# Gate and up projections of an encoder layer as seven block products instead of eight, with one pool of weight operands

## The chip, the cores and the metric

The kernel runs on one core of one Trainium2 chip. The time is the device time of one execution in microseconds (us); a kernel's time is the median of its runs. One execution was also taken by the hardware profiler, which gives each engine's instructions with start, duration and what released them. The engines are PE (TensorE: matmuls and transposes), DVE (VectorE), ACT (ScalarE), POOL (GpSimd) and SP (SyncE, which issues the DMA transfers). PEld is the loading of a matmul's stationary operand, which runs beside PE.

## The reference

One step of a streaming encoder layer for 640 tokens (512 of a prompt, 128 of eight samples), 1024 features, inner dimension 2816. What comes ahead of the change is attention; the tail is what the change touches:

```python
def layer_tail(x, ada, o_a, o_b, gates, w_o_a, w_o_b, w_out, g_norm_ffn, w_gate, w_up, w_down):
    shift1, scale1, gate1, shift2, scale2, gate2 = ada
    B, S = o_a.shape[:2]
    y_a = o_a.reshape(B, S, N_HEADS_A * V_DIM_A) @ w_o_a
    y_b = o_b.reshape(B, S, N_HEADS_B * HEAD_DIM_B) @ w_o_b
    x = x + gate1 * ((gates[:, :, 0] * y_a + gates[:, :, 1] * y_b) @ w_out)
    h = modulate(rmsnorm(x, g_norm_ffn), shift2, scale2)
    return x + gate2 * ((jax.nn.silu(h @ w_gate) * (h @ w_up)) @ w_down)
```

All tensors are fp32.

## The kernel before

Every large product is made of matmuls on pairs: an fp32 operand x is split into hi, a rounded copy that the matmul takes, and lo = x - hi. `split` (L83 to L89) makes the pair: ACT casts (L85), DVE subtracts (L86; POOL where the caller says so). `mm3` (L91 to L94) then issues three matmuls for one product, hi by hi, hi by lo, lo by hi. A `granule` (L178) is a weight piece of 128 partitions x 1024: SP loads it into a raw tile (three of them, tag w_raw), and `split` makes w_hi and w_lo (three of each in a pool).

The stages: conditioning terms, input projection and attention until about 594 us; the output projections of the two branches (L1086 to L1116), in four weight groups `bg`, until about 664; w_out with the residual (L1181 to L1201), two column halves c by five tiles of 128 tokens, until 721; the FFN from 726 to the end. Each stage's operands are in pools; `wstA` lives from the start, and `wstB2` beside it is opened after attention, so that the first `w_o_a` granule uses buffers of a pool that is open all along.

In the second column half of w_out, each token tile t goes through `h2_stats(t)` (L1140: sum of squares, reciprocal root, xn = x times it), then `h2_cols(t)` (L1149: eight transposes, scale and shift, split into h2T and h2Tl, the FFN's moving operands). Meanwhile the gate and up weights of FFN blocks 0 and 1 are loaded and split, with POOL making the lo part (`ff_weights(.., G)`).

The FFN goes through 22 blocks of 128 inner columns. `ff_block` (L1209) does one block for one half of the tokens (320 columns): 24 matmuls into a gate bank, silu on ACT (L1216), 24 into an up bank, a DVE product of the two (L1219), and a split into aT and aTl. A block takes 96 matmuls. The first two blocks do the first token half first, which does not need the last token tile. The blocks come in passes of 8, 8 and 6. After each pass the down projection adds to the residual (matmuls of 512 columns into one bank per tile and column half, L1250 and L1251 on DVE).

The order of each engine's instructions is fixed when the program is built, by a scheduler that mixes the stages where their operands allow; at run time each engine goes through its list in order and waits on semaphores. An engine that waits holds up all that stands behind it on its list.

Of the kernel before, what the change touches and what calls it, by code (L numbers as in the profile page):

```python
# [47 lines left out]
def layer_kernel(  # L48
# [42 lines left out]
    def mm3(out, lh, ll, rh, rl, start, stop):  # L91
        T.matmul(out, lh, rh, start=start, stop=False)  # L92
        T.matmul(out, lh, rl, start=False, stop=False)  # L93
        T.matmul(out, ll, rh, start=False, stop=stop)  # L94
# [67 lines left out]
    wa = ctx.enter_context(pool("wstA", side="right"))  # L162
# [884 lines left out]
    wb_cm = pool("wstB2", side="right")  # L1047
    wb = wb_cm.__enter__()
    AB = (wa, wb)
    gp_cm = pool("gatebc", side="right")  # L1050
    gp = gp_cm.__enter__()
# [12 lines left out]
    def gate_rows(c0, scale):  # L1064

        raw = ada_rows(c0)
        hi = wa.tile([P, 1024], F32R, tag="w_hi", bufs=3, name=nm("whi"))[0:19, :]
        lo = wa.tile([P, 1024], F32R, tag="w_lo", bufs=3, name=nm("wlo"))[0:19, :]
        split(hi, lo, raw)
        out = []  # L1070
        for v in range(2):
            g_ = gp.tile([P, DM], F32, tag=f"gate{v}", name=nm("gate"))
            for c in range(2):
                cc = slice(c * 512, (c + 1) * 512)
                ps = mm_tile()
                T.matmul(ps, selr[:, v * P:(v + 1) * P], hi[:, cc], start=True, stop=False)  # L1076
                T.matmul(ps, selr[:, v * P:(v + 1) * P], lo[:, cc], start=False, stop=True)  # L1077
# [4 lines left out]
    with pool("mwork") as mw:  # L1082
# [10 lines left out]
        for bg in range(4):  # L1093
            wo = [granule(AB[br], wo_v[br][:, :, bg * 256:(bg + 1) * 256], [4, 256]) for br in range(2)]
            for bl in range(2):
# [6 lines left out]
                for hf in range(2):  # L1102
                    c = slice(hf * HALF, (hf + 1) * HALF)
                    ts = []
                    for br in range(2):
                        ps = mm_tile()
                        for k in range(4):
                            ws = slice(bl * P, (bl + 1) * P)
                            mm3(ps[:, :HALF], wo[br][0][:, k, ws], wo[br][1][:, k, ws],
                                oS[br, hf][0][:, k, :], oS[br, hf][1][:, k, :], k == 0, k == 3)  # L1110
# [20 lines left out]
    h2T = h2p.tile([P, KD, NT], F32R, tag="h2T", name="h2T")  # L1131
    h2Tl = h2p.tile([P, KD, NT], F32R, tag="h2Tl", name="h2Tl")
# [4 lines left out]
    sq = ow.tile([P, 2, TT], F32, tag="sq", name="sq")  # L1137
    xns = {}
# [10 lines left out]
    def h2_cols(t):  # L1149
        tsl = slice(t * P, (t + 1) * P)  # L1150
        for b in range(2):
# [4 lines left out]
            hf_ = ow.tile([P, 512], F32, tag="hfull", bufs=2, name=nm("hfull"))  # L1156
# [14 lines left out]
            split(h2T[:, kb_, tsl], h2Tl[:, kb_, tsl], hf_.rearrange("p (k n) -> p k n", k=4))  # L1171
# [4 lines left out]
    def ff_weights(fb, eng=None):  # L1176
        cs_ = slice(fb * P, (fb + 1) * P)
        return granule(wa, wg_v[:, :, cs_], [KD, P], eng=eng) + granule(wb, wu_v[:, :, cs_], [KD, P], eng=eng)

    ffw = []  # L1180
# [128 lines left out]
```

## Time and profile before

| | |
|---|---|
| median of 3 runs | 1199.36 us (1196.3 to 1201.92) |
| profiled execution, its own time | 1195.43 us |
| its span in the trace | 1193.7 us |
| PE busy | 1163.5 us, 97% |
| DVE / ACT / POOL busy | 650.9 / 521.1 / 106.5 us (55 / 44 / 9%) |
| mean granted TensorE clock | 0.991 |
| DMA | 155.29 MB, mean 130 GB/s |

The span is cut into 40 slices; each digit is the busy share of a slice in tenths (9 is 90% or more). PEclk is the clock granted to TensorE in tenths of full speed (full is 2.4 GHz, half 1.2 GHz):

```profile
PE   8899999999999999999899998999999999999998
PEld 6578988999998788889699888999889999889996
DVE  4988555857887785555555256422343332433333
ACT  6766533446776664566643166322122222112210
POOL 2521001000000000112012221000000000000000
PEclk9999999999999999999989999999999999999999
```

Slices 25 to 40 are the FFN: PE is full, DVE and ACT have much room and POOL does nothing. A matmul's duration in the trace is longer than the distance between two starts, because matmuls overlap in the array; the pace of a stream is read from starts.

### The profile page before, as it was taken

The page shows a single profiled execution, that of the slowest core. Times are in us where ns is not written, and L with a number is a line of the kernel's source. Part 1 is how long each engine was busy: PE and PEld are TensorE (multiplying, and loading weights), DVE is VectorE, ACT ScalarE, POOL GpSimd, SP SyncE. Part 2 cuts the span into 40 slices and gives each one's busy share as a digit, 9 for nine tenths or more (in the row PEclk, how much of TensorE's full clock was granted, in tenths as well). Part 3 has the DMA queues.
Part 4 walks back from the last instruction along what each step waited for, and adds up shares of the span by engine and source line. Part 5 has one row for each costly group of instructions (what it writes and reads, how often), then busy time and mean ns, then how long its engine had stood idle before and what let it go on. Part 6 is the DMA issues. An engine that isn't in the chain of part 4 may idle for free. (4 is left out here: it accounts for less than half of the span.)

```text
span 1193.7 us, 19291 instructions
## 1 busy us (share of the span) xinstructions
PE 1163.5 (97%) x7427; PEld 1045.2 (88%) x7427; DVE 650.9 (55%) x1472; ACT 521.1 (44%) x1062; POOL 106.5 (9%) x188
## 2 busy tenths in 40 slices
PE   8899999999999999999899998999999999999998
PEld 6578988999998788889699888999889999889996
DVE  4988555857887785555555256422343332433333
ACT  6766533446776664566643166322122222112210
POOL 2521001000000000112012221000000000000000
PEclk9999999999999999999989999999999999999999
DMA  8732434567555445576676112322123222222211
GB/s 235 269 107 65 134 124 145 173 196 224 171 174 165 133 147 168 197 232 218 180 266 198 36 57 71 110 85 71 36 71 108 87 73 87 68 74 72 71 45 62
DMA packets 155166, 155.29 MB, mean 130 GB/s; under 512 B 24632, under 2 KB 115283, under 8 KB 155074
## 3 DMA queue, kind: packets, MB, share of 16 engines
q1 hardware_dynamic: 155074, 154.05, 41.6%
q8 instruction: 59, 0.97, 0.3%
q14 instruction: 33, 0.27, 0.1%
HBM read 135.15 MB, written 18.88 MB: 129 GB/s over the span
## 5 line engine op out<-in xcount | busy, mean ns | idle before, releaser
L85 ACT CAST whi<-wraw 128x1024 fp32r<-128x1024 f32 (+3 forms) x168 | 173.2, 1037 | 274.6 <-PE mm L94 108.0
L86 DVE TENSOR_TENSOR wlo<-wraw,whi 128x1024 fp32r<-128x1024 f32 (+3 forms) x152 | 182.5, 1203 | 134.4 <-ACT whi L85 131.3
L93 PE MATMUL mm<-h2Tl,whi 128*128 128x320 f32 x704 | 217.2, 309 | 0.0
L94 PE MATMUL mm<-h2T,wlo 128*128 128x320 f32 x704 | 217.1, 309 | 0.0
L92 PE MATMUL mm<-h2T,whi 128*128 128x320 f32 x704 | 216.8, 309 | 0.2 <-ACT h2T L85 0.2
L92 PEld LDWEIGHTS mm<-h2T,whi 128*128 128x128 f32 x704 | 131.9, 188 | 0.9 <-ACT h2T L85 0.4
L93 PEld LDWEIGHTS mm<-h2Tl,whi 128*128 128x128 f32 x704 | 132.1, 188 | 0.4 <-DVE h2Tl L86 0.3
L94 PEld LDWEIGHTS mm<-h2T,wlo 128*128 128x128 f32 x704 | 132.1, 188 | 0.0
L1219 DVE TENSOR_TENSOR sg<-mm,sg 128x320 f32<-128x320 f32 x44 | 21.6, 492 | 119.6 <-PE mm L94 117.5
L93 PE MATMUL mm<-wlo,aT 128*128 128x512 f32 x220 | 85.5, 389 | 0.0
L92 PE MATMUL mm<-whi,aT 128*128 128x512 f32 x220 | 85.5, 389 | 0.0
L94 PE MATMUL mm<-whi,aTl 128*128 128x512 f32 x220 | 85.4, 389 | 0.0
L92 PE MATMUL mm<-whi,hT_hi 128*128 128x512 f32 (+3 forms) x240 | 79.5, 332 | 2.5 <-ACT jk L320 2.5
L92 PE MATMUL mm<-hT_hi,whi 128*128 128x320 f32 x256 | 81.7, 319 | 0.0
L94 PE MATMUL mm<-whi,hT_lo 128*128 128x512 f32 (+3 forms) x240 | 79.6, 332 | 0.0
L94 PE MATMUL mm<-hT_hi,wlo 128*128 128x320 f32 x256 | 79.5, 311 | 0.0
L93 PE MATMUL mm<-hT_lo,whi 128*128 128x320 f32 x256 | 79.4, 310 | 0.0
L93 PE MATMUL mm<-wlo,hT_hi 128*128 128x512 f32 (+3 forms) x240 | 79.3, 331 | 0.0
L1250 DVE TENSOR_TENSOR tmp<-mm,gate 128x512 f32<-128x512 f32 x30 | 20.7, 691 | 79.9 <-PE mm L94 79.9
L85 ACT CAST aT<-sg 128x320 fp32r<-128x320 f32 x44 | 20.0, 455 | 77.2 <-DVE sg L1219 77.2
L92 PEld LDWEIGHTS mm<-whi,hT_hi 128*128 128x128 f32 x240 | 45.2, 188 | 6.5 <-ACT jk L320 2.9
L92 PEld LDWEIGHTS mm<-hT_hi,whi 128*128 128x128 f32 x256 | 48.2, 188 | 2.6 <-issue 1.7
(328 smaller groups left out, 2476.6 us busy)
## 6 DMA issues: line engine op xcount, KB each, us to landing
wraw<-in_w_ada_dram SPq DMA_DIRECT2D x48, 512.0 KB, 4.8
wraw<-in_w_in_dram SPq DMA_DIRECT2D x28, 512.0 KB, 4.6
wraw<-in_w_gate_dram SPq DMA_DIRECT2D x22, 512.0 KB
wraw<-in_w_up_dram SPq DMA_DIRECT2D x22, 512.0 KB, 3.9
wraw<-in_w_down_dram SPq DMA_DIRECT2D x22, 512.0 KB, 3.6
lat<-in_cache_kv_latent_dram SPq DMA_DIRECT2D x16, 512.0 KB, 5.7
wraw<-in_cache_band_v_dram SPq DMA_DIRECT2D x16, 512.0 KB, 5.2
kn<-in_cache_band_k_dram SPq DMA_DIRECT2D x16, 512.0 KB, 3.7
```

What stands on the lines that cost most here:

```text
L85: S.copy(hi, src)
L86: (eng or V).tensor_tensor(out=lo, in0=src, in1=f(hi), op=ALU.subtract)
L92: T.matmul(out, lh, rh, start=start, stop=False)
L93: T.matmul(out, lh, rl, start=False, stop=False)
L94: T.matmul(out, ll, rh, start=False, stop=stop)
L1219: V.tensor_tensor(out=sg, in0=pu[:, :HALF], in1=sg, op=ALU.mult)
L1250: V.tensor_tensor(out=tmp, in0=ps, in1=gate2[t // 4][:, cc], op=ALU.mult)
```

## The change

With the gate and up weights of one block as two rows of a 2x2 block matrix (gate over up; inner halves 1 and 2), and the activations as a 2x2 block matrix (inner halves by token halves), gate and up for all tokens are a 2x2 block product. It is done in seven products instead of eight. Each product has a weight operand of 128x512 and activations of 4 x 320 columns, so 12 matmuls; a block takes 84.

- The activations are kept as hB (three blocks: b11, b21, b22) and hS (four sums t1 to t4, made on POOL from each token tile, then split in four pieces of 128x1280 after the last tile). The two token halves are interleaved by 64 tokens within each tile.
- Per block POOL makes s1, s2, a21' and s4 from the raw weights (L1246 to L1249 of the new code), in one tile `sums`. Each of the seven operands is split on its own (ACT cast and DVE subtraction of 128x512).
- Partial results are shared between products in one PSUM bank: after a product into `pa`, ACT copies the bank (u1, u2, u3, L1260) and the next product adds on top of it. The tiles sums, u1, u2, u3 and u5 have one buffer each.
- All weights from the output projections on go through one pool, `wops`, with 12 pairs of 128x512 and the three raw tiles; the old pool is closed after attention. POOL no longer splits blocks 0 and 1; their weights are not loaded ahead by a call of their own. The rows of the last gate come ahead of the FFN. Passes are 6, 6, 6 and 4 blocks.

```diff
+    def mm3(out, lh, ll, rh, rl, start, stop, more=False):
...
     sb_cm.__exit__(None, None, None)
-    wb_cm = pool("wstB2", side="right")
-    wb = wb_cm.__enter__()
-    AB = (wa, wb)
+    wa_cm.__exit__(None, None, None)
+
+    wa = ctx.enter_context(pool("wops", side="right"))
+
+    def operand(src, n=512):
+        hi = wa.tile([P, 512], F32R, tag="op_hi", bufs=12, name=nm("ophi"))[:, :n]
+        lo = wa.tile([P, 512], F32R, tag="op_lo", bufs=12, name=nm("oplo"))[:, :n]
+        split(hi, lo, src)
+        return hi, lo
+
+    def operands(src, shape):
+        raw = load_raw(src, shape)[0]
+        return [operand(raw[:, i * 512:(i + 1) * 512]) for i in range(2)]
...
-            split(h2T[:, kb_, tsl], h2Tl[:, kb_, tsl], hf_.rearrange("p (k n) -> p k n", k=4))
+            quarter.append(hf_.rearrange("p (k a x) -> p a k x", k=4, a=2))
+        (b11, b12), (b21, b22) = [(h[:, 0], h[:, 1]) for h in quarter]
+        split(hB[0][:, 0, :, q], hB[1][:, 0, :, q], b11)
+        split(hB[0][:, 1, :, q], hB[1][:, 1, :, q], b21)
+        split(hB[0][:, 2, :, q], hB[1][:, 2, :, q], b22)
+        t1, t2, t3, t4 = [hT_[:, i, :, q] for i in range(4)]
+        for o, a, b in ((t1, b12, b11), (t2, b22, t1), (t3, b22, b12), (t4, b21, t2)):
+            G.tensor_tensor(out=o, in0=a, in1=b, op=ALU.subtract)
...
-                if t in (1, 3):
-                    ffw.append(ff_weights(len(ffw), G))
     h2_cols(4)
     mT_cm.__exit__(None, None, None)
+    tsum = ctx.enter_context(pool("tsum", side="right"))
+    hS = [tsum.tile([P, 4, 4, HALF], F32R, tag=f"hS{i}", name=f"hS{i}") for i in range(2)]
+    for i in (1, 0, 2, 3):
+        split(hS[0][:, i], hS[1][:, i], hT_[:, i])
...
+        def ff_block(fb, fi):
+            raw = ff_raw(fb)
+            (a11, a12), (a21, a22) = [(r[:, 0:512], r[:, 512:1024]) for r in raw]
+            sums = fw.tile([P, 3, 512], F32, tag="sums", name=nm("sums"))
+            s1, s2, s4 = sums[:, 0], sums[:, 1], sums[:, 2]
+            G.tensor_tensor(out=s1, in0=a21, in1=a22, op=ALU.add)
+            G.tensor_tensor(out=s2, in0=s1, in1=a11, op=ALU.subtract)
+            G.tensor_tensor(out=a21, in0=a11, in1=a21, op=ALU.subtract)
+            G.tensor_tensor(out=s4, in0=a12, in1=s2, op=ALU.subtract)
+
+            def product(bank, w, h, i, start=True):
+                wh, wl = operand(w)
+                for k in range(4):
+                    ks = slice(k * P, (k + 1) * P)
+                    mm3(bank[:, :HALF], wh[:, ks], wl[:, ks], h[0][:, i, k, :], h[1][:, i, k, :],
+                        start and k == 0, k == 3, not start)
+
+            def part(bank, tag):
+                o = fw.tile([P, HALF], F32, tag=tag, name=nm(tag))
+                S.copy(o, bank[:, :HALF])
+                return o
+
+            pa, pc, pb = mm_tile(), tr_tile(), (mm_tile if fb % 2 else tr_tile)()
+            product(pa, a11, hB, 0)
+            u1 = part(pa, "u1")
+            product(pc, a12, hB, 1)
+            V.tensor_tensor(out=u1, in0=pc[:, :HALF], in1=u1, op=ALU.add)
+            S.activation(out=u1, in_=u1, func=AF.Silu)
+            product(pa, s2, hS, 1, start=False)
+            u2 = part(pa, "u2")
+            product(pb, s1, hS, 0)
+            u5 = part(pb, "u5")
+            product(pa, a21, hS, 2, start=False)
+            u3 = part(pa, "u3")
+            G.tensor_tensor(out=u3, in0=u3, in1=u5, op=ALU.add)
+            product(pb, s4, hB, 2, start=False)
+            V.tensor_tensor(out=u2, in0=pb[:, :HALF], in1=u2, op=ALU.add)
+            S.activation(out=u2, in_=u2, func=AF.Silu)
+            product(pa, a22, hS, 3, start=False)
+            V.tensor_tensor(out=u1, in0=pa[:, :HALF], in1=u1, op=ALU.mult)
+            G.tensor_tensor(out=u2, in0=u2, in1=u3, op=ALU.mult)
+            for i, u in enumerate((u1, u2)):
+                o = [a[:, fi].rearrange("p (t a x) -> p t a x", a=2, x=64)[:, :, i, :] for a in (aT, aTl)]
+                split(o[0], o[1], u.rearrange("p (t x) -> p t x", x=64))
```

How the instructions stand on the engines, at three places. In the rows, a line number is followed by the operation, what it writes, what it reads, its shape, and the semaphores on which it waits.

First PE in the second pass of the FFN. Before, a block for one token half: the last matmuls into the gate bank (`mm_10555`), and the first into the up bank (`mm_10556`):

```order
L92 MATMUL mm_10555<-h2T,whi_10490 128x320
L93 MATMUL mm_10555<-h2Tl,whi_10490 128x320
L94 MATMUL mm_10555<-h2T,wlo_10491 128x320
L92 MATMUL mm_10556<-h2T,whi_10496 128x320 [waits DVE_49]
L93 MATMUL mm_10556<-h2Tl,whi_10496 128x320
L94 MATMUL mm_10556<-h2T,wlo_10497 128x320
```

Now, in the second pass too (block 11): the product of s2 (`ophi_11080`) ends, and the product of a21' (`ophi_11116`) into the same bank follows it at once:

```order
L93 MATMUL mm_11041<-hS_9132,ophi_11080 128x320
L94 MATMUL mm_11041<-hS_9133,ophi_11080 128x320
L95 MATMUL mm_11041<-hS_9132,oplo_11081 128x320
L93 MATMUL mm_11041<-hS_9132,ophi_11116 128x320 [waits Activation_49]
L94 MATMUL mm_11041<-hS_9133,ophi_11116 128x320
L95 MATMUL mm_11041<-hS_9132,oplo_11117 128x320
```

Where the bank used to change between two products, the second now goes into the bank that ACT has yet to copy.

ACT around the same place. Before, silu of a gate bank (`sg`), the casts of the next weights (`whi`) and of the result (`aT`):

```order
L1216 ACTIVATE sg_10526<-mm_10500 128x320 [waits PE_49,Activation_49]
L85 CAST aT_10364<-sg_10526 128x320 [waits DVE_49]
L85 CAST whi_10856<-wraw_10854 128x1024 [waits DMAHW6_49,PE_49]
L1216 ACTIVATE sg_10581<-mm_10555 128x320 [waits PE_49,Activation_49]
L85 CAST whi_10862<-wraw_10860 128x1024 [waits DMAHW7_49,PE_49]
L85 CAST aT_10364<-sg_10581 128x320 [waits DVE_49]
```

Now; `u_2402` is u1 of block 11, `u_2407` its u2 and `u_2413` its u3, and `ophi_11327` to `ophi_11337` are operands of the down projection:

```order
L85 CAST ophi_11327<-wraw_11325 128x512 [waits DMAHW0_49,PE_49]
L1260 COPY u_2402_11060<-mm_11041 128x320 [waits DVE_49]
L1268 ACTIVATE u_2402_11060<-u_2402_11060 128x320 [waits DVE_49]
L85 CAST ophi_11331<-wraw_11325 128x512 [waits PE_49]
L1260 COPY u_2407_11096<-mm_11041 128x320 [waits PE_49]
L1278 ACTIVATE u_2407_11096<-u_2407_11096 128x320 [waits DVE_49]
L85 CAST ophi_11337<-wraw_11335 128x512 [waits DMAHW1_49,PE_49]
L1260 COPY u_2413_11132<-mm_11041 128x320 [waits PE_49]
```

A weight cast that waits for PE stands ahead of each copy that PE waits for.

DVE at the end of w_out, the last token tile. Before:

```order
L1169 TENSOR_TENSOR hfull_9037<-tr_9032,A_87 128x512 [waits PE_49]
L1169 TENSOR_TENSOR hfull_9047<-tr_9042,A_87 128x512 [waits PE_49]
L1170 TENSOR_TENSOR hfull_9037<-hfull_9037,B_88 128x512 [waits DVE_49]
L1170 TENSOR_TENSOR hfull_9047<-hfull_9047,B_88 128x512 [waits DVE_49]
L86 TENSOR_TENSOR h2Tl<-hfull_9037,h2T 128x4x128 [waits Activation_49]
L86 TENSOR_TENSOR h2Tl<-hfull_9047,h2T 128x4x128 [waits Activation_49]
```

Now; `hB_8541` and `hS_9133` are the lo parts of hB and hS:

```order
L1188 TENSOR_TENSOR hfull_9107<-hfull_9107,B_88 128x512 [waits DVE_49]
L1187 TENSOR_TENSOR hfull_9115<-tr_9110,A_87 128x512 [waits PE_49,Pool_49]
L86 TENSOR_TENSOR hB_8541<-hfull_9107,hB_8540 128x4x64 [waits Activation_49]
L1188 TENSOR_TENSOR hfull_9115<-hfull_9115,B_88 128x512 [waits DVE_49]
L86 TENSOR_TENSOR hS_9133<-hsum,hS_9132 128x1280 [waits Activation_49]
L86 TENSOR_TENSOR hB_8541<-hfull_9115,hB_8540 128x4x64 [waits Activation_49] x2
L86 TENSOR_TENSOR hS_9133<-hsum,hS_9132 128x1280 [waits Activation_49] x3
L1267 TENSOR_TENSOR u_2086_9205<-tr_9187,u_2086_9205 128x320 [waits PE_49,Activation_49]
```

A large subtraction of 1280 columns now stands ahead of those that the second product needs, three more ahead of the first addition for u1 (`u_2086`), and the first FFN product needs the last token tile.

## Rows read from the trace of the kernel before

**Rows 1.** The page's part 1, the whole span: engine, busy us, share, instructions

```profile
PE 1163.5 (97%) x7427; PEld 1045.2 (88%) x7427; DVE 650.9 (55%) x1472; ACT 521.1 (44%) x1062; POOL 106.5 (9%) x188
```

**Rows 2.** Four stretches: length, busy us (x instructions) by engine, PEclk, DMA share, GB/s

```profile
596.00:601.00 5.00, 2.71 (x21) 2.48 (x20) 3.53 (x7) 4.84 (x14) 0.00 (x0) 0.93 0.65 196
601.00:607.00 6.00, 6.00 (x23) 5.97 (x24) 3.52 (x7) 1.89 (x2) 0.00 (x0) 0.50 0.67 215
721.00:726.00 5.00, 1.53 (x11) 0.99 (x10) 4.97 (x10) 3.51 (x8) 1.23 (x1) 1.00 0.42 115
726.00:1189.00 463.00, 462.96 (x2788) 435.75 (x2788) 165.31 (x229) 109.32 (x168) 0.00 (x0) 1.00 0.25 75
```

**Rows 3.** PE's groups by line, 726 to 1189: busy us, mean ns

```profile
L94 PE MATMUL mm<-h2T,wlo 128*128 128x320 f32 x704 | 217.1, 309 | 0.0
```

**Rows 4.** Timeline, blocks 2 on: start us, us, engine line op; idle before, releaser

```profile
802.32 0.31 PE L94 MATMUL mm<-h2T,wlo 128*128 128x320 f32 x1
...
803.21 0.31 PE L94 MATMUL mm<-h2T,wlo 128*128 128x320 f32 x1
...
803.61 0.44 ACT L1216 ACTIVATE sg<-mm 128x320 f32<-128x320 f32 x1 [2.32 <-PE mm L94]
...
804.52 0.31 PE L94 MATMUL mm<-h2T,wlo 128*128 128x320 f32 x1
```

**Rows 5.** ACT's groups with shapes, 664 to 1194: busy us, mean ns, idle before

```profile
L85 ACT CAST whi<-wraw 128x1024 fp32r<-128x1024 f32 x69 | 72.5, 1051 | 217.7 <-PE mm L94 106.2 <-PE mm L93 88.0 <-DMA wraw<-in_w_up_dram 12.5
...
L1216 ACT ACTIVATE sg<-mm 128x320 f32<-128x320 f32 x44 | 19.1, 434 | 42.4 <-PE mm L94 42.4
...
L85 ACT CAST h2T<-hfull 128x512 fp32r<-128x512 f32 x10 | 5.8, 619 | 0.6 <-DVE hfull L1170 0.6
```

**Rows 6.** DVE's groups with shapes, 664 to 1194

```profile
L1219 DVE TENSOR_TENSOR sg<-mm,sg 128x320 f32<-128x320 f32 x44 | 21.6, 492 | 119.6 <-PE mm L94 117.5 <-ACT sg L1216 2.0
L86 DVE TENSOR_TENSOR aTl<-sg,aT 128x320 fp32r<-128x320 f32 x44 | 21.5, 489 | 12.1 <-ACT aT L85 12.1
...
L86 DVE TENSOR_TENSOR h2Tl<-hfull,h2T 128x512 fp32r<-128x512 f32 x10 | 6.5, 687 | 0.7 <-ACT h2T L85 0.6
```

**Rows 7.** POOL's groups with shapes, 590 to 1194

```profile
L1115 POOL TENSOR_TENSOR t<-t,t 128x320 f32<-128x320 f32 x16 | 15.9, 996 | 66.1 <-DVE t L1112 41.9 <-DMA x<-in_x_prompt_dram 24.2
...
L1194 POOL TENSOR_TENSOR x<-x,tmp 128x512 f32<-128x512 f32 x5 | 6.5, 1296 | 15.8 <-DVE tmp L1193 15.8
```

**Rows 8.** POOL's timeline at the end of w_out

```profile
717.49 4.74 POOL L86 TENSOR_TENSOR wlo<-wraw,whi 128x1024 fp32r<-128x1024 f32 x2 [20.30 <-ACT whi L85]
```

**Rows 9.** DVE's timeline beside it

```profile
718.06 1.84 DVE L1143 TENSOR_TENSOR ss<-sq 128x1 f32<-128x1 f32 x1 [0.45 <-ACT tmp L1195]
...
720.46 1.78 DVE L107 TENSOR_TENSOR rst<-rs 128x1 f32<-128x1 f32 x1
```

**Rows 10.** Line 1143 alone: durations in ns, least, median, most

```profile
L1143 DVE TENSOR_TENSOR ss<-sq x5: 152/159/1840, 699.3 to 727.5; 128x1 f32<-128x1 f32 x5
```

**Rows 11.** PE's timeline where the FFN begins

```profile
720.91 0.39 PE L94 MATMUL mm<-whi,mTl 128*128 128x512 f32 x1
724.59 1.09 PE L138 MATMUL tr<-ident,xn 128*128 128x128 f32 x8 [3.29 <-ACT xn L1146]
725.87 0.86 PE L92 MATMUL mm<-h2T,whi 128*128 128x320 f32 x4 [0.18 <-ACT h2T L85]
```

**Rows 12.** ACT's timeline, the last token tile

```profile
732.85 1.15 ACT L1146 ACTIVATE xn<-x,rs 128x1024 f32<-128x1024 f32 x1
```

**Rows 13.** DVE's timeline, the last token tile

```profile
739.78 1.29 DVE L86 TENSOR_TENSOR h2Tl<-hfull,h2T 128x512 fp32r<-128x512 f32 x2
```

**Rows 14.** SP's queue before the output projections

```profile
585.49 0.78 SPq L168 DMA_DIRECT2D wraw<-in_w_o_a_dram  x1
...
591.97 1.77 SPq L1100 DMA_DIRECT2D g<-gate_d  x4
```

**Rows 15.** PE's timeline, first output-projection product

```profile
594.13 0.42 PE L92 MATMUL mm<-oh,whi 128*128 128x320 f32 x1
```

More of the change, by code (lines that the diff above doesn't have):

```diff
@@ L89, in split @@
             (eng or V).scalar_tensor_tensor(out=lo, in0=src, scalar=scale, in1=f(hi), op0=ALU.mult, op1=ALU.subtract)
[L91 to L94, printed above, removed]
+    def mm3(out, lh, ll, rh, rl, start, stop, more=False):
+        T.matmul(out, lh, rh, start=start, stop=False, skip_group_check=more)
+        T.matmul(out, lh, rl, start=False, stop=False, skip_group_check=more)
+        T.matmul(out, ll, rh, start=False, stop=stop, skip_group_check=more)
     def rsqrt(out, ss, inv, pl, n):
@@ L159, in layer_kernel @@
     e_d = dram.tile([H, ESZ], F32, tag="e_d", name="e_d")
-    wa = ctx.enter_context(pool("wstA", side="right"))
+    wa_cm = pool("wstA", side="right")
+    wa = wa_cm.__enter__()
     def load_raw(src, shape, rows=P):
@@ L1093, in layer_kernel @@
         for bg in range(4):
-            wo = [granule(AB[br], wo_v[br][:, :, bg * 256:(bg + 1) * 256], [4, 256]) for br in range(2)]
+            wo = [operands(wo_v[br][:, :, bg * 256:(bg + 1) * 256], [4, 256]) for br in range(2)]
             for bl in range(2):
@@ L1184, in layer_kernel @@
         for g in range(4):
-            hi, lo = granule(AB[g % 2], w_out_v[:, 2 * g:2 * g + 2, cc], [2, 512])
-            ws += [(hi[:, j, :], lo[:, j, :]) for j in range(2)]
+            ws += operands(w_out_v[:, 2 * g:2 * g + 2, cc], [2, 512])
         for t in range(TT):
@@ new lines, in layer_kernel @@
+    tsum = ctx.enter_context(pool("tsum", side="right"))
+    hS = [tsum.tile([P, 4, 4, HALF], F32R, tag=f"hS{i}", name=f"hS{i}") for i in range(2)]
+    for i in (1, 0, 2, 3):
+        split(hS[0][:, i], hS[1][:, i], hT_[:, i])
+    ow_cm.__exit__(None, None, None)
+    wd_v = w_down[0].rearrange("(k p) n -> p k n", p=P)
+    gate2 = gate_rows(5 * DM, 1.0)
+    NB = 6
+    with pool("fwork") as fw:
+        def ff_block(fb, fi):
[39 more added lines that the diff above has]
+                split(o[0], o[1], u.rearrange("p (t x) -> p t x", x=64))
+        for f0 in range(0, NFF, NB):
+            f1 = min(f0 + NB, NFF)
+            nf = f1 - f0
+            aT = fw.tile([P, NB, NT], F32R, tag="aT", name=nm("aT"))
+            aTl = fw.tile([P, NB, NT], F32R, tag="aTl", name=nm("aTl"))
+            for fb in range(f0, f1):
+                ff_block(fb, fb - f0)
```

68 lines of the change are left out of this document (20 added, 48 removed).

## The prediction

> **What bounds the kernel now.** I read the page's totals first: PE is busy 97% of the span and no other engine over 55% [rows 1]. Then the FFN as a stretch of its own: from 726 to 1189 PE is busy 462.96 of 463.00 us at full clock, while DVE has 165, ACT 109 and POOL nothing [rows 2]. So the FFN lasts as long as its matmuls, and fewer matmuls shorten it, as long as the others keep PE fed. Gate and up take three groups of 704 matmuls of 320 columns, one of which stands in [rows 3]: 2112 = 22 blocks x 96. Their 309 ns is not their pace. In the timeline the matmuls that start at 802.32 and 804.52 are fifteen apart [rows 4]: 2.20/15 = 0.147 us each.
>
> **What is removed.** 84 instead of 96 matmuls in each of 22 blocks: 264 fewer, 264 x 0.147 = **-38.8 us**. All of it is on the path, since PE is never idle there.
> The Trainium skill ("TensorE: Matmul & The Clock Gate", Back-to-back issue gap) gives N/2.4 + 2.5 ns for an isolated warm matmul, 136 ns for 320 columns. The trace shows 147, so it differs; by the page the saving would be 35.9 us and the forecast 2.9 later. I take the trace.
>
> **What is added on PE's path: hand-offs of a bank.** Before, silu reads a gate bank while PE fills another: the copy costs PE nothing. Now u1, u2 and u3 are copied by ACT out of the bank into which the next product goes, so PE waits unless another product stands between. In PE's list I counted the matmuls between each pair. Most pairs have 1.76 us (one product) or more. None stands between s2 and a21' in three blocks of each of passes 1 to 3, nor between a21' and a22 in one block of each; the last pass has three such places. That is 3 x 4 + 3 = 15. The price: the last matmul of a bank starts at 803.21, ACT's read of it at 803.61 [rows 4], so 0.40; the read takes 0.434 [rows 5]; PE starts 0.08 after ACT ends (my allowance; ACT's hop to PE is under 0.2). That is 0.91 instead of 0.147: 0.77 lost. At most of the fifteen ACT has a weight cast ahead of the copy, which waits for an operand buffer that the same product frees; it takes 0.619 [rows 5] and starts one matmul before the bank is done, so it adds 0.5: 1.3 lost. 15 x 1.3 = **+19.5**. Bounds: 15 x 0.77 = 11.6; with two casts ahead, 15 x 1.87 = 28. Behind the waiting cast stand the copy, silu and all later casts; PE waits for the copy at once, for the casts only after the 12 operands in store.
>
> Where one product (12 x 0.147 = 1.76) stands between, 1.3 fits, so those cost nothing. Two longer chains are closer to their cover. u1 has one buffer: a22 of one block, DVE's product 0.492 [rows 6], ACT's cast, DVE's subtraction 0.489 [rows 6], then the copy of the next u1, then s2: 0.4 + 0.49 + 0.45 + 0.49 + 0.43 and four hops, 2.7 to 3.5 us, against 3.1 to 3.5 us of other matmuls in nine blocks. I take **+4** (bounds 0 and 10). One operand per pass is cast with 1.8 us to spare: **+1.5** (0 to 3).
>
> **Supply of operands.** Per block ACT has seven casts of 0.62, four copies and two silus of about 0.43, and two casts of aT: 7.9 us of the 12.35 that 84 matmuls take. DVE has 7 x 0.687 + 2 x 0.489 = 5.8 of operations with two SBUF inputs, and three on PSUM of 0.49; POOL has four of 512 columns at 1.296 and two of 320 at 1.0 [rows 7], together 7.2. Each alone fits. But they do not run side by side here: while POOL subtracts from 717.49 to 722.23 [rows 8], two DVE additions of one column take 1.84 and 1.78 us [rows 9], where line 1143 otherwise takes 0.159 [rows 10]. The two together need 5.8 + 7.2 = 13.0 us a block, over the 12.35; with DVE's PSUM work of 1.5 behind it 14.5. Against that stands the down projection: in a pass of six it gives PE 180 matmuls of 512 columns with no POOL work, and the list of PE mixes it among the blocks; also PE's own stalls give 0.9 us a block. I take the exclusion to cost only the lateness that is in the +4 above; its other end is a rival.
> The Trainium skill ("GPSIMD Engine Reference", 1. Specifications) says that POOL shares its SBUF interface with DVE, with contention where DVE has two SBUF inputs. It speaks against this change, which gives POOL 132 operations that it did not have; the trace agrees (1.84 against 0.159), and the rival is priced from it.
>
> **The start of the FFN.** Before, PE idles 3.29 us ahead of the last-but-one tile's transposes [rows 11] and then begins the FFN's first token half, under which tile 4 (the last) is prepared: its last subtraction ends at 741.07 [rows 13], 20.2 us after the last w_out matmul at 720.91 [rows 11]. Now nothing of the FFN can begin before tile 4. Its chain by durations alone is about 9 to 10 us (two DVE operations and a square of 0.6 to 0.7, seven short ones of 0.16, xn 1.15 [rows 12], transposes 1.09 [rows 11], two more of 0.69, a cast, a subtraction, hops); with tile 3's work among it, as before, I put the first product at 15 us after 720.91. Then DVE has an hS piece of 1280 columns (about 1.5, from 0.687 at 512 and 0.489 at 320) ahead of the hB pieces that the second product needs, three more ahead of the addition for u1, ACT three hS casts and a table load ahead of silu, and s1's and s2's casts come after silu. So PE has two products, waits, has the next two from about 25 us on, and begins a21' of block 0 at 29 us. By then it has done five products (8.8 us) and eight gate matmuls with the transposes (3.5): 16.5 us of waiting, against 3.5 before. A fall of the clock comes on top: after 596 to 601, when PE was busy 2.71 of 5 us, the granted clock was 0.50 (1.2 GHz) for 6.00 us [rows 2], worth 3 us; after 721 to 726, busy 1.53 of 5, it stayed at 1.00 [rows 2]. I take **+14** for the whole; bounds 8 (first product at 10 us, no fall) and 20.
>
> **The output projections.** Before, `w_o_a` is issued at 585.49, ahead of the four gate loads at 591.97 [rows 14], and PE starts the products at 594.13 [rows 15]. Now the operands take buffers of a pool that opens only when attention's is closed, and on SP both loads stand behind the gate loads: issue at about 594.2, about 5 us to land, cast and subtraction 1.3: ready near 600.5. Before, PE did only 16 matmuls before waiting from about 596.5 to 599 for another load, which stays. So 16 matmuls move behind that wait, at the low clock: **+2.7** (0 to 5). Other weights have 12 pieces of 512 as store, as large as before; DMA is a quarter busy in the FFN [rows 2].
>
> **Sum.** -38.8 + 19.5 + 4 + 1.5 + 14 + 2.7 = +2.9, on the profiled execution's 1195.43: 1198.3. That execution is 3.9 below the median of the runs, and the changed kernel will be timed by such runs: **1202**.
>
> **Rivals.**
> *Faster: the hand-offs are cheap.* The casts' buffers come free earlier, each hand-off is 0.77, the start costs 8 and the u1 chain nothing: -38.8 + 11.6 + 8 + 1.5 + 2.7 = -15, 1180.4 + 3.9 = 1184. For it: copies read a bank within 0.4 of its last matmul, and the lists leave room elsewhere. Against: the cast stands ahead on ACT's list, and cannot be passed.
> *Slower: POOL and DVE set the pace.* A block needs 14.5 us of the two, PE with its stalls has 13.2, so 1.3 a block are lost from the point where the operands in store are used up; 22 x 1.3 = 29, less what the down projections let them catch up, about half: +14.5, 1217. For it: [rows 9]; against: no row shows DVE's long operations under POOL at this rate, and the down projection gives slack.
> *The clock falls again and again.* Each fall costs 3 us [rows 2]; one a pass and some more, eight in all, would be +24, 1226. Against: 3.29 us of idle at 721 brought none.
> *The seven products do not save PE time,* if starts of shorter accumulations were farther apart: then nothing is gained and the sum is +42, 1241. Nothing in the trace speaks for it: the pace does not change between banks [rows 4].
>
> **Chances.** The gain about used up, within 0.5% (6 us, about what a measurement of this kernel can tell from no change; 1193.4 to 1205.4): 0.36. Faster than that: 0.33, most of it between 1180 and 1193. Slower: 0.31, of which POOL and DVE have 0.2, a start or hand-offs at their upper ends 0.07, the rest 0.04. The forecast's own range is 1194 to 1210; adding up all low ends gives 1180, all high ones 1226. The range reaches to 1183 and 1218.
>
> **What would show it.** In the new profile: 1848 matmuls of 320 columns in the FFN's products, 0.147 apart; some fifteen stalls of PE of 0.8 to 1.9 us released by ACT's copy; a gap of 15 us or more between the last w_out matmul and the FFN's steady stream; the first w_o load after 594. The forecast is wrong if PE's waits in the FFN are released by casts or subtractions of operands (the slower rival), or add up to under 12 us (the faster one), or if the start costs under 8.

## The result, and the profile after

The changed kernel takes 1214.82 us (median of 4 runs, 1213.51 to 1215.46) against 1197.83 for the kernel before in the same runs: ratio 1.0141, 95% interval 1.0112 to 1.017. It is slower by 17 us. The forecast was 1202, with a range of 1183 to 1218.

The page's part 1 after (columns as in [rows 1]), and the busy slices of PE with its clock:

```profile
PE 1143.5 (94%) x7163; PEld 1013.3 (84%) x7163; DVE 781.0 (65%) x1677; ACT 610.9 (50%) x1309; POOL 291.7 (24%) x336
...
PE   7899999999999999999799995988999999999998
...
PEclk9999999999999999999899996999999999999999
```

PE has 264 instructions fewer than in [rows 1] and is busy 20 us less, but the span is 1210.5 instead of 1193.7, so PE waits more. The slices say where: one near 600 us and, above all, those between 725 and 815. The windows (columns as in [rows 2]) put numbers on it:

```profile
728.00:745.00 17.00, 8.79 (x34) 6.80 (x34) 15.97 (x26) 12.92 (x25) 10.64 (x12) 0.60 0.00 0
745.00:752.00 7.00, 0.65 (x2) 0.63 (x3) 4.07 (x5) 3.42 (x7) 3.88 (x4) 0.77 0.00 0
752.00:811.00 59.00, 54.29 (x339) 52.62 (x339) 43.51 (x54) 30.54 (x62) 38.09 (x27) 0.94 0.33 99
811.00:850.00 39.00, 34.33 (x196) 30.61 (x196) 16.81 (x27) 16.27 (x35) 10.91 (x10) 1.00 0.26 81
850.00:912.00 62.00, 61.91 (x347) 55.80 (x346) 41.75 (x57) 23.05 (x44) 24.59 (x18) 1.00 0.25 72
```

The whole account, from the starts of PE's matmuls: every gap between two starts, less the pace of the matmul before it (0.147 us for 320 columns, 0.227 for 512), is waiting or slowness.

| stretch | before | after | difference | forecast |
|---|---|---|---|---|
| last product of attention to last output projection | 69.84 | 74.02 | +4.2 | +2.7 |
| w_out | 57.08 | 57.07 | 0 | 0 |
| last w_out matmul to last matmul of all | 467.82 | 481.03 | +13.2 | |
| - 264 matmuls fewer | | | -38.8 | -38.8 |
| - losses until the first FFN product | 3.9 | 10.2 | +6.3 | with the next: |
| - losses from there to 87 us after w_out | 0.7 | 19.1 | +18.4 | +14 + 4 + 1.5 |
| - fifteen hand-offs (14 x 1.05 + 0.68) | 0 | 15.4 | +15.4 | +19.5 |
| - four ends of passes | 0 | 4.7 | +4.7 | 0 |
| - pace of 660 down matmuls | 0 | 4.0 | +4.0 | 0 |
| - smaller gaps after that | -0.6 | 2.6 | +3.2 | 0 |

With 0.6 us less in attention and at the end, that is the 16.8 between the two spans.

**A hand-off.** PE's and ACT's timelines around a21' of a block in the second pass (columns as in [rows 4]):

```profile
947.06 0.31 PE L95 MATMUL mm<-hS,oplo 128*128 128x320 f32 x1
948.26 0.41 PE L93 MATMUL mm<-hS,ophi 128*128 128x320 f32 x1 [0.89 <-ACT u L1260]
```

```profile
947.26 0.62 ACT L85 CAST ophi<-wraw 128x512 fp32r<-128x512 f32 x1 [2.30 <-PE mm L94]
947.78 0.42 ACT L1260 COPY u<-mm 128x320 f32<-128x320 f32 x1
```

The bank's last matmul starts at 947.06 and the next product at 948.26: 1.20 instead of 0.147, so 1.05 lost. The cast is there as forecast, released by the matmul before the last (L94); it starts 0.20 after the last one's start, and the copy 0.52 after the cast.

**The start of the FFN.** PE, then ACT, POOL and DVE:

```profile
735.40 1.97 PE L139 MATMUL tr<-ident,xn 128*128 128x128 f32 x8 [6.29 <-ACT xn L1163]
738.53 0.63 PE L93 MATMUL mm<-hB,ophi 128*128 128x320 f32 x1 [1.16 <-ACT hB L85]
...
751.35 0.64 PE L93 MATMUL mm<-hS,ophi 128*128 128x320 f32 x1 [6.58 <-ACT ophi L85]
```

```profile
748.00 0.42 ACT L1260 COPY u<-mm 128x320 f32<-128x320 f32 x1 [2.99 <-DVE hS L86]
748.44 1.28 ACT L1268 ACT_TABLE_LOAD   x1
...
750.68 1.14 ACT L85 CAST ophi<-sums 128x512 fp32r<-128x512 f32 x2 [0.47 <-POOL sums L1247]
```

```profile
748.04 1.26 POOL L1246 TENSOR_TENSOR sums<-wraw 128x512 f32<-128x512 f32 x1 [4.62 <-issue]
```

```profile
743.62 4.28 DVE L86 TENSOR_TENSOR hS<-hsum,hS 128x1280 fp32r<-128x1280 f32 x3
```

The first product starts 13.95 us after the last w_out matmul (724.59). The second long wait is not the order on ACT that I had read: ACT stands idle 2.99 us ahead of u1's copy, and POOL 4.62 ahead of the first weight sum. Both begin when DVE's last hS piece ends (747.90), though POOL's row names no releaser: the tiles u1 and sums lie in the space of the pool that holds hsum, which hS is made from, and that space is free only then (e2_start below tests this).

**The end of a pass.** PE, DVE and POOL:

```profile
970.16 0.50 PE L93 MATMUL mm<-ophi,aT 128*128 128x512 f32 x1 [1.11 <-DVE u L1280]
```

```profile
968.64 1.06 DVE L86 TENSOR_TENSOR aTl<-u,aT 128x320 fp32r<-128x320 f32 x1 [3.60 <-ACT aT L85]
969.62 0.48 DVE L1280 TENSOR_TENSOR u<-mm,u 128x320 f32<-128x320 f32 x1
```

```profile
968.07 1.28 POOL L1247 TENSOR_TENSOR sums<-sums,wraw 128x512 f32<-128x512 f32 x1
```

By the trace the down projection's next bank waits for DVE's last product of the block, and that comes late: the subtraction ahead of it takes 1.06 instead of 0.489 [rows 6], because POOL works until 969.35.

**The pace of the down projection.** The group of its first matmul, before and after (page, part 5, columns as in [rows 3]):

```profile
L92 PE MATMUL mm<-whi,aT 128*128 128x512 f32 x220 | 85.5, 389 | 0.0
```

```profile
L93 PE MATMUL mm<-ophi,aT 128*128 128x512 f32 x220 | 87.8, 399 | 4.4 <-DVE u L1280 4.0
```

The starts are 0.226 to 0.227 apart before, and 0.231 to 0.232 and 0.235 by turns after, with the same shapes.

**The clock.** Part of the table's differences is slower matmuls and not waiting. First the kernel before, then the changed one (columns as in [rows 2]):

```profile
607.20:664.00 56.80, 56.27 (x377) 54.65 (x376) 31.40 (x57) 18.78 (x29) 14.21 (x15) 1.00 0.61 206
```

```profile
608.80:636.00 27.20, 27.20 (x188) 26.77 (x187) 19.10 (x37) 11.95 (x23) 6.77 (x7) 1.00 0.58 188
636.10:639.40 3.30, 3.30 (x15) 3.30 (x14) 2.20 (x6) 0.47 (x2) 1.18 (x1) 0.50 0.72 218
748.80:755.50 6.70, 4.15 (x15) 4.04 (x16) 4.32 (x6) 5.06 (x9) 4.68 (x4) 0.50 0.07 20
796.60:799.90 3.30, 3.30 (x14) 3.30 (x14) 2.35 (x3) 2.28 (x5) 1.39 (x1) 0.50 0.38 110
```

At 0.50 (1.2 GHz) the starts of 320-column matmuls are 0.26 to 0.27 apart instead of 0.147. The stretch at 636, in the output projections, costs about 1.6 us; PE had been busy without a pause for the 27.20 us before it, and the kernel before has no such stretch. After w_out the clock is at 0.50 three times (from 728 to 742, and the last two rows); 35 matmuls at that pace are about 4 us of the 6.3 + 18.4.

### The profile page after: what moved, and what is told of

Read it like the earlier page. It is cut to its first block, busy times and chain, and to the rows that moved or that the text cites. A ratio compares the mean times of both kernels' runs of the same rounds, so it can differ in the third digit from the quotient of the medians.

```text
span 1210.5 us, 19525 instructions
## 1 busy us (share of the span) xinstructions
PE 1143.5 (94%) x7163; PEld 1013.3 (84%) x7163; DVE 781.0 (65%) x1677; ACT 610.9 (50%) x1309; POOL 291.7 (24%) x336
## 4 chain that ended last, share of the span: by engine, by line
PE 81%; ACT 4%; DVE 4%; DMA 4%; POOL 3%; issue 2%; SPq 1%; POOLq 0%; ACTq 0%; DVEq 0%
PE mm L93 21%; PE mm L94 20%; PE mm L95 20%; PE tr L139 6%; PE mm L200 2%; PE mm L201 2%; PE tr L95 2%; PE tr L93 2%; PE tr L94 2%; DMA wraw<-in_w_up_dram 2%; DMA wraw<-in_w_ada_dram 1%; PE mm L924 1%; ACT ophi L85 1%; PE mm L776 1%; POOL sums L1249 1%
## 5 line engine op out<-in xcount | busy, mean ns | idle before, releaser
L86 DVE TENSOR_TENSOR oplo<-wraw,ophi 128x512 fp32r<-128x512 f32 (+1 forms) x168 | 134.5, 812 | 97.5 <-ACT ophi L85 97.1
L85 ACT CAST ophi<-wraw 128x512 fp32r<-128x512 f32 (+1 forms) x168 | 102.3, 620 | 174.4 <-PE mm L95 77.1
L93 PE MATMUL mm<-hS,ophi 128*128 128x320 f32 x308 | 97.7, 318 | 22.1 <-ACT u L1260 15.6
L85 ACT CAST whi<-wraw 128x1024 fp32r<-128x1024 f32 (+2 forms) x84 | 85.2, 1024 | 39.6 <-DMA wraw<-in_w_ada_dram 13.8
L86 DVE TENSOR_TENSOR wlo<-wraw,whi 128x1024 fp32r<-128x1024 f32 (+2 forms) x72 | 84.5, 1179 | 26.2 <-ACT whi L85 23.3
L95 PE MATMUL mm<-hS,oplo 128*128 128x320 f32 x308 | 96.3, 313 | 1.1 <-DVE oplo L86 1.1
L94 PE MATMUL mm<-hS,ophi 128*128 128x320 f32 x308 | 96.0, 312 | 0.0
L93 PE MATMUL mm<-ophi,aT 128*128 128x512 f32 x220 | 87.8, 399 | 4.4 <-DVE u L1280 4.0
L94 PE MATMUL mm<-oplo,aT 128*128 128x512 f32 x220 | 87.0, 396 | 0.0
L95 PE MATMUL mm<-ophi,aTl 128*128 128x512 f32 x220 | 84.4, 396 | 0.0
L93 PEld LDWEIGHTS mm<-hS,ophi 128*128 128x128 f32 x308 | 58.5, 190 | 27.4 <-ACT u L1260 20.0
L94 PE MATMUL mm<-wlo,hT_hi 128*128 128x512 f32 (+3 forms) x240 | 79.9, 333 | 0.0
L94 PE MATMUL mm<-hT_lo,whi 128*128 128x320 f32 x256 | 79.4, 310 | 0.0
L1246 POOL TENSOR_TENSOR sums<-wraw 128x512 f32<-128x512 f32 x22 | 31.5, 1430 | 124.4 <-DMA wraw<-in_w_up_dram 63.5
L94 PEld LDWEIGHTS mm<-hS,ophi 128*128 128x128 f32 x308 | 58.6, 190 | 0.6
```

The lines of the kernel that those rows point to most:

```text
L85: S.copy(hi, src)
L86: (eng or V).tensor_tensor(out=lo, in0=src, in1=f(hi), op=ALU.subtract)
L93: T.matmul(out, lh, rh, start=start, stop=False, skip_group_check=more)
L94: T.matmul(out, lh, rl, start=False, stop=False, skip_group_check=more)
L95: T.matmul(out, ll, rh, start=False, stop=stop, skip_group_check=more)
L1246: G.tensor_tensor(out=s1, in0=a21, in1=a22, op=ALU.add)
```

## The experiments

Ratios are to the kernel before, measured in the same runs. Each edit is to the changed kernel. "Losses" are those of the table: up to the first FFN product, from there to 87 us after w_out, and later (10.2, 19.1 and 26.8 in the changed kernel).

**1. e1_pin: the products in the order of the code**

```diff
-        T.matmul(out, lh, rh, start=start, stop=False, skip_group_check=more)
+        first = T.matmul(out, lh, rh, start=start, stop=False, skip_group_check=more)
+        if pin:
+            tc.keep_in_program_order(first)
...
-                        start and k == 0, k == 3, not start)
+                        start and k == 0, k == 3, not start, pin=k == 0)
```

So the first matmul of each of the seven products is held in the code's order.

> The only edit: on PE the seven products of all blocks stay in the order in which the code names them, so s1 stands between s2 and a21', s4 between a21' and a22 (no hand-off without a product of 1.76 us between; the changed kernel has fifteen). Theory (the waits for ACT's copy are the largest new cost in the steady FFN): the sixteen stalls of about 1.05 us go, 16 us, and new waits for operands come to at most 4: ratio to the kernel before about 1.002 (1.000 to 1.006). Rival (POOL and DVE set the pace of operands): the stalls move to the operands of the products, and the time changes by less than 4 us: 1.011 to 1.016.

Measured: 1194.11 us, ratio 0.999 (0.9978 to 1.0002), 18 us less than the changed kernel. All hand-off stalls are gone, the pass-end stalls with them, which I had not counted; later losses fall from 26.8 to 3.9, while those of the first blocks rise from 19.1 to 22.7. The window after the first blocks:

```profile
801.00:1168.00 367.00, 366.75 (x2156) 340.41 (x2157) 212.09 (x320) 159.35 (x316) 141.84 (x106) 1.00 0.26 78
```

PE is busy 366.75 of 367 us beside DVE's 212 and POOL's 142. So the hand-offs were the scheduler's choice of order, and POOL and DVE do not set the pace: the rival falls for the steady FFN, if not by much, since the two add up to 354 of the 367 us. In the first blocks it does show. One wait is 5.8 us at 766; ACT's copy of u1 waits for DVE, which takes 3.01 us for two subtractions that take 0.489 each alone [rows 6]:

```profile
771.90 0.43 ACT L1262 COPY u<-mm 128x320 f32<-128x320 f32 x1 [4.92 <-DVE aTl L86]
```

```profile
769.99 3.01 DVE L86 TENSOR_TENSOR aTl<-u,aT 128x320 fp32r<-128x320 f32 x2
```

**2. e2_start: sums and u1 in a pool of their own**

```diff
+    fwu = ctx.enter_context(pool("fwu", side="right"))
...
-            sums = fw.tile([P, 3, 512], F32, tag="sums", name=nm("sums"))
+            sums = fwu.tile([P, 3, 512], F32, tag="sums", name=nm("sums"))
...
-                o = fw.tile([P, HALF], F32, tag=tag, name=nm(tag))
+                o = (fwu if tag == "u1" else fw).tile([P, HALF], F32, tag=tag, name=nm(tag))
```

> The only edit: the tiles sums and u1 lie in a pool of their own and not in the space that hsum (the sources of hS) holds until all four hS pieces are split. Theory (the start of the FFN is long because the first block's weight sums and u1 wait for that space, and so the casts of s1 and s2 stand behind the hS casts, a table load and silu): PE's wait of 6.7 us ahead of s2 of block 0 falls to 1 to 3, and some of the waits up to 810 us go: 5 to 10 us less than the changed kernel, ratio to before 1.006 to 1.010. Rival (the hS pieces themselves bound it): under 2 us, 1.012 to 1.014.

Measured: 1206.80, ratio 1.0093 (1.0075 to 1.0111), 8 us less. The 6.7 us wait ahead of s2 is gone, but the first product now starts 20.9 us after w_out instead of 13.9, since operands of two blocks are made ahead of the last token tile (c3_start below bears on this). Losses 17.1, 6.9 and 25.9: the first two together 24.0 instead of 29.2. The shared space was a cause, worth 5 us by these losses and 8 by the medians; the last tile's chain stays.

**3. e3_raw_open: raw tiles open from the start**

```diff
+    wr = ctx.enter_context(pool("wraw", side="right"))
     wa_cm = pool("wstA", side="right")
...
-        raw = wa.tile([P, 1024], F32, tag="w_raw", bufs=3, name=nm("wraw"))
+        raw = wr.tile([P, 1024], F32, tag="w_raw", bufs=3, name=nm("wraw"))
```

> The only edit: the three raw tiles lie in a pool that stays open from the start, so the first loads of the output projections can be issued during attention; hi and lo still wait for the new pool. Theory (the load that stands behind the gate loads is what costs at 594): the first output-projection product starts at 594 to 596 and not at 598.1, and the time falls by 2 to 4 us: ratio to before 1.010 to 1.012. Rival (the wait is for the space of hi and lo, or for the other load that stops PE in both kernels): under 1 us.

Measured: 1211.91, ratio 1.0135 (1.0113 to 1.0157): inside its interval the same as the changed kernel. The stretch up to the last output projection takes 72.56 instead of 74.02 (69.84 before). SP's queue and ACT show why it is not more:

```profile
585.50 0.68 SPq L171 DMA_DIRECT2D wraw<-in_w_o_a_dram  x1
```

```profile
592.17 4.42 ACT L85 CAST oh<-oT 128x320 fp32r<-128x320 f32 x12
...
598.77 2.18 ACT L85 CAST ophi<-wraw 128x512 fp32r<-128x512 f32 x4
```

The load is issued as early as in [rows 14], but its casts stand behind the twelve of `oh` and what follows them, since hi and lo still wait for the new pool. The first product started at 601.90, behind sixteen small transposes that PE had waited for a load to make, and not at 594 to 596 as the theory had it. The 1.46 us are a third of the 4.2: that much was the load, and the rival was nearer.

**4. e4_right: aT at the other end of the memory**

```diff
-    with pool("fwork") as fw:
+    with pool("fwork", side="right") as fw:
```

> The only edit: the pool of aT, aTl and the small FFN tiles is taken from the other end of the memory, as in the kernel before. The down projection's 660 matmuls of 512 columns start 0.231 and 0.235 us apart by turns in the changed kernel, 0.227 before. Theory A (the pace depends on where aT lies): back to 0.227, 4 us less, ratio to before 1.010 to 1.012. Theory B (POOL's and DVE's work beside it, or the order of the matmuls): the pace stays at 0.231 to 0.235 and the time within 1.5 us of the changed kernel's.

Measured: 1209.20, ratio 1.0122 (1.0098 to 1.0146), 4 us less in the spans; the interval overlaps that of the changed kernel, so the pace has to decide. The starts are mostly 0.226 to 0.227 apart again, and the last group of the down projection, after and in this kernel:

```profile
L95 PE MATMUL mm<-ophi,aTl 128*128 128x512 f32 x220 | 84.4, 396 | 0.0
```

```profile
L95 PE MATMUL mm<-ophi,aTl 128*128 128x512 f32 x220 | 83.1, 389 | 0.0
```

The order of instructions on PE, ACT, DVE and POOL is the same in both traces, so the pace hangs on where the pool lies (theory A).

**5. e7_pad32, e8_pad64, e9_pad96: what in the address?**

```diff
+        pad = fw.tile([P, 8], F32, tag="pad", name="pad")
+        V.memset(pad, 0.0)
```

e8_pad64 and e9_pad96 have 16 and 24 in place of 8.

> The changed kernel with aT and aTl moved up by 32 bytes per partition (a pad of eight fp32 ahead of them, on the same side of the memory): from addresses that are multiples of 64 to ones that leave 32, as all weight operands and the kernel before's aT do. Theory (the pace of the down projection's matmuls hangs on that offset of 32): 0.227 us a matmul as with the other end of the memory, about 3 to 4 us less than the changed kernel, ratio to before 1.010 to 1.012. Rival (the end of the memory or the distance from the operands): the pace stays at 0.231 to 0.235.

> As e7_pad32 with a pad of 64 bytes, so that the offset stays a multiple of 64. Theory (offset of 32): the pace of the down projection stays at 0.231 and 0.235 by turns. Rival (any shift): 0.227.

> The changed kernel with a pad of 96 bytes ahead of aT and aTl. With pads of 0, 32 and 64 bytes (addresses that leave 0, 32, 64 over a multiple of 128) the down projection's matmuls start 0.230 to 0.238 us apart; at the other end of the memory, and in the kernel before, where the address leaves 96 as all weight operands' do, 0.227. Theory (the pace hangs on that remainder of 96): 0.227 with this pad, on the old side of the memory, and 3 to 4 us less than the changed kernel, ratio to before 1.009 to 1.012. Rival (the side of the memory or the distance): 0.230 or more, time as the changed kernel's.

Measured: e7 1212.48 (ratio 1.0145, 1.012 to 1.017), e8 1212.9 in one run, e9 1214.26 (1.0145, 1.0116 to 1.0174). The pace stays: medians 0.233, 0.234 and 0.232, with other patterns of gaps. e9, whose offset is that of the fast kernels by the program's addresses:

```profile
L95 PE MATMUL mm<-ophi,aTl 128*128 128x512 f32 x220 | 84.2, 395 | 0.0
```

Both offset theories fall. That the place of the pool decides is shown by e4, and c1, c2 and c3 with the same place have 0.226 to 0.227 too. Whether it is the side of the memory, the distance from the other operand or something else in the address stays open: no run parts these.

**6. e5_nosum: without POOL's four sums**

```diff
-            sums = fw.tile([P, 3, 512], F32, tag="sums", name=nm("sums"))
-            s1, s2, s4 = sums[:, 0], sums[:, 1], sums[:, 2]
-            G.tensor_tensor(out=s1, in0=a21, in1=a22, op=ALU.add)
...
+            s1, s2, s4 = a22, a21, a12
```

> The changed kernel without POOL's four weight sums per block: the operands s1, s2, a21', s4 are plain pieces of the raw weights instead (so gate and up are not computed; matmuls, splits and copies stay as many). Rival from the prediction (POOL's 88 sums, which lock DVE out, set the pace of the FFN): 10 us or more less than the changed kernel, ratio to before 1.006 or less. Theory (in the steady FFN nothing waits for them; they matter only in the first blocks, up to 810 us): the fifteen hand-offs of 1.05 us and the wait at the end of each pass stay, the early waits shrink by 4 to 7 us: ratio 1.008 to 1.011.

Measured: 1200.99, ratio 1.0038 (1.0023 to 1.0053): as low as the rival's figure, 13.1 us less in the spans. Where it went speaks against the rival's place, though. Losses are 14.0, 5.5 and 23.9: 9.7 us come from the first four blocks and the last token tile, 2.9 from later (the pass ends fall from 1.29 to 0.75). The fifteen hand-offs stay at 14 x 1.05 and 0.68. So POOL's sums cost some 12 us here, but most of it at the start, where DVE has the last tile's work, all of hS and the first operands to do while POOL holds it off. Not all of the 9.7 is POOL's work: this kernel has no tile `sums` that waits for space. e2_start, which takes away that wait and u1's alone, had 24.0 in the first two losses; here they are 19.5, so 4.5 us are beyond the space. My theory had the place right and half the size.

**7. e6_eight: the new structure with eight products**

```diff
-            product(pa, a11, hB, 0)
-            u1 = part(pa, "u1")
...
+            for j in range(2):
+                banks = []
+                for r in range(2):
+                    bank = (mm_tile, tr_tile)[r]()
+                    for h in range(2):
...
+                S.activation(out=u, in_=banks[0][:, :HALF], func=AF.Silu)
+                V.tensor_tensor(out=u, in0=banks[1][:, :HALF], in1=u, op=ALU.mult)
```

Here j goes over the token halves, r over gate and up (a bank each), h over the inner halves; there are no sums.

> The structure of the change with the old product: pool of 512-column operands, passes of 6, token halves interleaved, aT at its new place, but eight products per block (96 matmuls) on b11, b12, b21, b22, no sums, no copies out of a bank in use; aT halves as before. It computes the whole reference. Theory (gain 38.8 us; costs: hand-offs 16, start 17, output projections 3.7, down pace 4, pass ends 4.7): of the costs the output projections, the pace and part of the start (the wait for tile 4, about 10) stay: 16 to 20 us over before, ratio 1.013 to 1.017, so the seven products by themselves win about nothing in this order. Rival (the start is long because of the sums t1 to t4 and hS): start as before, ratio 1.006 to 1.009.

Measured: 1215.11, ratio 1.0153 (1.0133 to 1.0173), the changed kernel's time. From the first product on PE waits for nothing:

```profile
743.00:1180.00 437.00, 436.92 (x2644) 412.39 (x2645) 165.67 (x273) 113.51 (x212) 0.00 (x0) 0.99 0.23 69
```

The losses are 11.7 up to the first product, 2.3 (slow matmuls, no waits) and 3.6 later. So the structure alone (one pool opened late, interleaved token halves, passes of six, aT's place) costs 18 us: 4.3 in the output projections, 9.4 up to 87 us after w_out and 4.2 later. In the changed kernel the seven products win back just what their own sums, copies and order cost. Theory held.

**8. c1_all and c2_u1: the four edits together; u1 with two buffers**

c1 has edits 1 to 4; c2 adds

```diff
-                o = (fwu if tag == "u1" else fw).tile([P, HALF], F32, tag=tag, name=nm(tag))
+                o = (fwu if tag == "u1" else fw).tile([P, HALF], F32, tag=tag, bufs=2 if tag == "u1" else 1, name=nm(tag))
```

> All four edits tried so far together: products in the order of the code on PE, sums and u1 in a pool of their own, raw tiles open from the start, aT at the other end of the memory. If they add up: 18 + 7 + 1 + 4 = 30 us less than the changed kernel's 1214.8, and some of the early waits go twice, so about 1186; ratio to before 0.987 to 0.992.

> As c1_all, with two buffers for u1. Theory (with the products in order, u1's single buffer is held by the block before until DVE has subtracted aT, behind POOL: the wait of 5.8 us at 766 in the kernel with the order alone): 3 to 7 us less than c1_all where that wait is still there, ratio 0.983 to 0.988. Rival (the casts of operands are late there anyway): within 2 us of c1_all.

Measured: c1 1177.91, ratio 0.9839 (0.9815 to 0.9863); c2 1176.00, ratio 0.9826 (0.9804 to 0.9849). Both beat the kernel before, by 19 and 21 us. c1 is below the 0.987 to 0.992 that I expected, where I took some of the early waits to be counted twice. By the profiled executions the four edits save 19.7, 6.8, 0.6 and 4.0 us, 31.1 together, and c1 saves 32.6: they add up. The losses are 17.1, 6.5 and 0.2, so with the space free the order no longer costs anything in the first blocks (22.7 in e1_pin). c2 is within 2 us of c1, as its rival said, but not for the rival's reason: in c1 the wait of 5.8 us at 766 is already gone. PE in c2 after the first blocks:

```profile
808.00:1152.00 344.00, 344.00 (x2026) 321.03 (x2026) 196.25 (x302) 147.64 (x292) 133.76 (x100) 1.00 0.26 78
```

344 of 344 us with DVE at 196 and POOL at 134.

**9. c3_start: POOL's sums of block 1 behind the last tile**

```diff
-            G.tensor_tensor(out=s1, in0=a21, in1=a22, op=ALU.add)
+            first = G.tensor_tensor(out=s1, in0=a21, in1=a22, op=ALU.add)
+            if fb == 1:
+                tc.keep_in_program_order(first)
```

> As c2_u1, and POOL's sums of block 1 held behind the last token tile's hsum on POOL's list. Theory (between 723 and 730 in c2_u1 these sums lock DVE out of the last tiles' norm and columns, so that the FFN's first product starts 20.9 us after the last w_out matmul, where it was 14): first product 14 to 17 us after it, 3 to 6 us less than c2_u1, ratio to before 0.977 to 0.980. Rival (the casts and subtractions of operands delay the last tile as much): first product still at 19 or later and under 2 us gained.

Measured: 1179.59, ratio 0.9862 (0.9837 to 0.9888), not better than c2. The first product does start 14.67 us after w_out, as the theory said, but the losses go from 17.1 and 6.3 to 10.9 and 15.5: the sums are late for the next blocks. ACT's casts wait for them, its copies stand behind the casts, and PE waits for the copies, as here:

```profile
772.13 0.62 ACT L85 CAST ophi<-sums 128x512 fp32r<-128x512 f32 x1 [1.56 <-POOL sums L1255]
...
774.93 0.41 ACT L1266 COPY u<-mm 128x320 f32<-128x320 f32 x1
```

```profile
775.40 0.42 PE L93 MATMUL mm<-hS,ophi 128*128 128x320 f32 x1 [2.52 <-ACT u L1266]
```

What was saved ahead of the first product was given back behind it. It looks as if in this stretch the whole of DVE's and POOL's work counts and not its order, but no run shows that.

## Why the prediction was right or wrong

The time lies in the range, and the likeliest mechanism (the gain used up by waits that the new order brings) held. But its band, up to 1205.4, was missed: the time is 13 us over the forecast, on the slower side, which I gave 0.31, and most of that for POOL and DVE, which do not set the pace of the steady FFN. In the spans the forecast was +2.9 and the result +16.8. The 13.9 between are 5.2 at the start, 4.7 and 4.0 for two terms that the sum did not have, 3.2 of smaller gaps and 1.5 in the output projections, less 4.1 at the hand-offs and 0.6 elsewhere. That the range held all this is partly luck. Term by term:

- **Saved matmuls, -38.8: right.** 1848 matmuls at a pace of 0.147, also in c2, where nothing else disturbs it. The isolated-gap figure that I had weighed against it does not show here.
- **Hand-offs, +19.5: right in number and cause, 15.4 in size.** Fifteen, as counted in PE's list; e1_pin removes them by order alone. The price was 1.05, between my 0.77 and 1.3: the cast begins 0.20 after the last matmul's start, not 0.25 to 0.4, and the copy follows it with an overlap of 0.10.
- **Start of the FFN and the u1 chain, +14 + 4 + 1.5: too small, and this is the step of the sum that failed.** It measured +24.7. The first product came at 13.95, as forecast (15). But I read the second wait from the order on ACT alone and missed what the diff shows: sums and u1 lie in memory that is free only when the last hS piece is split (e2_start: 5 to 8 us). And I priced POOL's lock of DVE at nothing there, though [rows 9] came from just ahead of this stretch; e5_nosum gives 9.7 us for the sums in the start and the first blocks, the space among them, and 4.5 beyond the space. The term also had one fall of the clock, 3 us, where three came.
- **Supply of operands by POOL and DVE:** the rival on the slower side gave 1217, close to the result, and its +14.5 is close to the 13.1 us that go with the sums in e5_nosum. But it had them in every block once the store of operands is used up, and the runs have most of them in the start and the first blocks: with the order pinned PE is 100% busy beside the two later on. The lock is real: two subtractions that take 0.489 each alone took 3.01 us. The Trainium skill (GPSIMD Engine Reference, 1. Specifications) states that POOL shares its SBUF interfaces with DVE, with contention where a DVE instruction has two SBUF inputs; the trace agrees. That the down projection's slack carries the 13.0 us a block of the two against 12.35, as the argument against the rival had it, fits the 354 of 367 us in e1_pin; no run tests it alone. Of the two operations in [rows 9] only the first is an addition; the second, of line 107, is a multiplication.
- **Output projections, +2.7: 4.2 in size, and right only in part.** The loads were issued at 593.84 and 594.27, as forecast, and PE's first product came at 598.09. But the gate loads were not what held them: these had been issued by 589.63, and SP then waited 4.1 us for PE's last matmuls of attention. Before, twelve matmuls and not sixteen ran ahead of the wait for the other load. And about 1.6 us are the second fall of the clock, at 636, which I did not foresee.
- **Left out: ends of passes, 4.7, and the pace of the down projection, 4.0.** The prediction names neither. The first was to be read from the order: DVE's product, POOL's lock and the bank's next user stand there. The second no row of the kernel before could show; I had not asked what the move of aT's pool from one side of the memory to the other does.
- **The clock falls:** more often than the sum allowed, and less often than the rival had it. It was at 0.50 three times between 728 and 800, where one fall was allowed for, and once more at 636. It stayed at 1.00 from 811 to the last matmul, through the stalls of 1 us. What brought it down at 636 and at 796, no run shows.

## What to carry to other kernels

Fewer matmuls can be used up by the waits that the new products bring. Look in PE's list for two neighbours that share a bank which another engine reads in between, and pin the order if the scheduler leaves no product between them (18 us here). That alone brought this kernel back to the time before (0.999); the gain came when the space, the place and the first loads were put right as well (0.984). When pools are closed and opened between stages, ask of each new tile whose space it takes and when that is free; a stage that may not start before then loses more than its order shows. Work that is hidden in the steady part is not hidden at the seam, where the last tile's chain, the first operands and the new sums meet on the same engines.

## What the runs showed of the hardware that was not expected

- The same 512-column matmuls start 0.227 us apart or 0.231 to 0.235, by the place of the pool that holds their stationary operand: 4 us over 660 matmuls. Shifts of 32, 64 and 96 bytes do not cure it (medians 0.232 to 0.234), taking the pool from the other side of the memory does.
- In the changed kernel's trace 28 of DVE's 44 subtractions of 128x320 for aTl have no POOL instruction beside them and take 0.48 to 0.50 us; the other 16 take 1.06 to 1.58. Once the order was pinned, this cost PE nothing in the steady FFN.
- The granted clock was at 0.50 from 636.1 to 639.4 after 27.2 us in which PE was busy throughout at 1.00. The kernel before and c1, c2 and c3 have no such stretch there; the cause is open.
